# The FFN's down product as seven block products instead of plain accumulation, with its weight operands made a phase earlier

## The chip, the cores and the metric

One core of one Trainium2 chip runs the whole program. The metric is the device time of one execution in microseconds (us). A program's time is the median of several executions; one further execution was recorded by the hardware profiler, and all durations below are from that one.

## What is computed

One decoder layer on 1032 tokens (1024 of a prompt, 8 single samples), with model width 1024 and FFN width 2816. Cut to what the change touches:

```
x = x + 1/2 * SwiGLU_1(RMSNorm(x))     # gate, up = split(x @ w_in); (silu(gate) * up) @ w_out
x = x + token_mix(RMSNorm(x))          # attention and gated DeltaNet, one output projection
x = x + 1/2 * SwiGLU_2(RMSNorm(x))
y = RMSNorm(x)
```

The two FFNs have the same shapes. The change is in the last product of each, `(silu(gate) * up) @ w_out`: 2816 hidden features (22 blocks of 128) into 1024 model features (8 blocks of 128), for all 1032 tokens.

## The kernel before, in words

**Number format.** Every matrix product works on a pair of tiles, hi and lo: ScalarE casts the fp32 value to hi, VectorE subtracts hi from it to get lo (`split`, L250). A product is three matmuls, hi x hi, hi x lo and lo x hi, into one PSUM bank (`mm3`, L319). Activations are stored with features on the 128 partitions and tokens along the free dimension.

**Gate and up** (`ffn_in`, L651). The gate and up columns of one block f of hidden features are two block rows, the tokens are cut into two halves p = 0, 1 and each half into two quarters of 258 columns, and the 2x2x2 block product is done with seven block products in place of eight (Strassen's scheme in Winograd's form). The operands of the tokens are made once for all f (`x_ops`) and hold 28 of the 44 work tiles (`SLOTS`) until the last f. Those of the weights are made for every f (`w_ops`, L478): GpSimd makes four sums or differences of 128x512, ScalarE and VectorE split seven of them into hi and lo; `A_LIVE` = 9 of these tiles may be alive. `product` (L519) issues 12 matmuls of 258 columns for each of the seven and each half. `swiglu` (L536) empties the banks on VectorE and ScalarE, multiplies on GpSimd, and writes the result h to memory (the DRAM tile `hd`).

**Down** (`ffn_out`, L706). h comes back by block (`h_tile`, L677: one load of 128x1032, one cast, one subtraction). The 22 blocks of hidden features are taken in five groups (`KGROUPS`, L37: 4, 4, 6, 4 and 4). For every group, output block m and chunk of 344 tokens, the group's blocks are accumulated in one bank and VectorE adds half of it to the residual x (`one`, L709). The weights are loaded as they stand in memory and split (`issue`, L296). Nothing but loads, casts, subtractions on VectorE and these additions goes on beside it. The last group of four runs chunk by chunk, with the norm that follows behind it.

**What sets the order.** TensorE runs in the order in which the program is written (`ORDERED`). Where another engine's instruction stands in its queue is decided by a scheduler that plays the program on a timeline of its own; once it stands there, each queue is worked in order. All DMAs named here are issued by SP's queue. Work tiles come from one list of 44 slots: a tile's first writer waits for the last user of the slot before. `adv` (L418) steps the builders of operands between products; a builder steps on while the free slots it asks for (`room`) are there.

## Time and profile before

| what | value |
|---|---|
| median of 3 runs | 2116.67 us (2114.2 to 2116.69) |
| the profiled execution: its time | 2115.43 us |
| the profiled execution: first to last instruction | 2113.2 us |
| TensorE (PE) busy, matmuls | 96% of the span, 15062 |
| VectorE (DVE), ScalarE (ACT), GpSimd (POOL) busy | 58%, 33%, 28% |
| mean granted TensorE clock | 0.973 of full speed |
| DMA over the span | 86 GB/s |

The gate-and-up phases fill about 139 to 509 us and 1465 to 1849 us of the span, the down products the 249 us behind each. In the rows below, a group reads: line, engine, operation, out<-in by the program's names, sizes, count | busy us, mean ns of one | idle time before it and what ended it. In a timeline row the first two numbers are start and duration in us. In a row of windows, each engine has its busy us and (x) its number of instructions; the last three columns are the granted TensorE clock, the DMA engines' mean busy share and GB/s. PEld is TensorE's weight load.

### The profile page before, as it was taken

What the parts mean: (1) busy time and instruction counts of PE and PEld (TensorE: products, weight loads), DVE (VectorE), ACT (ScalarE), POOL (GpSimd) and SP (SyncE); (2) the same over time, 40 slices, a digit from 0 to 9 for tenths busy, and PEclk for the clock granted to TensorE, in tenths of its full rate; (3) what the DMA queues carried; (4) which work ended last, traced back from release to release, by engine and by line L of the source; (5) the groups of instructions that cost most, each with busy time, mean ns of one, the idle gap of its engine ahead of it and who ended that gap; (6) DMA issues with size and microseconds to landing.
All of it is one profiled execution on the core that took longest, in us unless ns stands there. A gap on an engine that the chain in (4) does not pass through costs nothing.

```text
span 2113.2 us, 37138 instructions
## 1 busy us (share of the span) xinstructions
PE 2024.6 (96%) x15062; PEld 1963.6 (93%) x15062; DVE 1222.1 (58%) x2624; ACT 699.8 (33%) x1491; POOL 594.9 (28%) x517
## 2 busy tenths in 40 slices
PE   7799999999999999999999979999999999999997
PEld 6799999999999998787888869899999999999997
DVE  7755555555533544676977874685555555464335
ACT  5233333333211333545243332443333333331112
POOL 3354444341000131332211111245444444200003
PEclk7999999999999999999999979999999999999999
DMA  4112222227322221211212151221222222552112
GB/s 152 60 58 91 81 73 84 86 71 281 113 68 60 84 81 35 69 45 32 67 46 50 57 181 35 97 70 61 86 81 83 79 81 76 194 195 84 55 41 81
DMA packets 109771, 180.81 MB, mean 86 GB/s; under 512 B 35168, under 2 KB 63744, under 8 KB 109584
## 3 DMA queue, kind: packets, MB, share of 16 engines
q1 hardware_dynamic: 109568, 178.41, 26.6%
q8 instruction: 118, 1.93, 0.4%
q14 instruction: 53, 0.43, 0.1%
q0 software_dynamic: 32, 0.03, 0.0%
HBM read 135.60 MB, written 43.85 MB: 85 GB/s over the span
## 4 chain that ended last, share of the span: by engine, by line
PE 40%; DVE 8%; DMA 1%; issue 1%; SPq 1%; ACT 0%; POOL 0%; DVEq 0%; ACTq 0%; POOLq 0%
PE mm L321 6%; PE mm L322 6%; PE mm L323 6%; PE ps L528 4%; PE ps L530 4%; PE ps L529 4%; PE ps L243 3%; PE mm L528 2%; PE mm L530 2%; PE mm L529 2%; DVE conv L89 1%; DVE inv L89 1%; SPq L102 1%; DVE Tb L89 1%; DVE x L89 1%
## 5 line engine op out<-in xcount | busy, mean ns | idle before, releaser
L528 PE MATMUL ps<-xhi,wop 128*128 128x258 f32 x1480 | 421.0, 284 | 7.4 <-DVE sw L89 7.2
L530 PE MATMUL ps<-xhi,wop 128*128 128x258 f32 x1480 | 419.3, 283 | 0.0
L529 PE MATMUL ps<-xlo,wop 128*128 128x258 f32 x1480 | 419.3, 283 | 0.0
L321 PE MATMUL mm<-hhi,hi 128*128 128x344 f32 x1008 | 322.3, 320 | 0.0
L322 PE MATMUL mm<-hlo,hi 128*128 128x344 f32 x1008 | 322.3, 320 | 0.0
L323 PE MATMUL mm<-hhi,lo 128*128 128x344 f32 x1008 | 321.6, 319 | 0.0
L89 DVE TENSOR_TENSOR wop<-r,wop 128x512 fp32r<-128x512 f32 x185 | 158.5, 859 | 253.9 <-ACT wop L89 239.8
L528 PEld LDWEIGHTS ps<-xhi,wop 128*128 128x128 f32 x1480 | 280.9, 190 | 8.7 <-issue 7.2
L529 PEld LDWEIGHTS ps<-xlo,wop 128*128 128x128 f32 x1480 | 281.9, 191 | 0.0
L530 PEld LDWEIGHTS ps<-xhi,wop 128*128 128x128 f32 x1480 | 281.2, 190 | 0.0
L89 DVE SCALAR_TENSOR_TENSOR x<-mm,x 128x344 f32<-128x344 f32 x240 | 123.3, 515 | 220.0 <-PE mm L323 217.9
L89 ACT CAST hi<-raw 128x1024 fp32r<-128x1024 f32 (+1 forms) x78 | 76.7, 984 | 357.0 <-PE mm L322 327.0
L321 PEld LDWEIGHTS mm<-hhi,hi 128*128 128x128 f32 x1008 | 189.4, 188 | 0.3 <-DVE x L89 0.3
L323 PEld LDWEIGHTS mm<-hhi,lo 128*128 128x128 f32 x1008 | 189.4, 188 | 0.0
L322 PEld LDWEIGHTS mm<-hlo,hi 128*128 128x128 f32 x1008 | 189.3, 188 | 0.0
L89 POOL TENSOR_TENSOR acc<-acc,t 128x344 f32<-128x344 f32 (+1 forms) x50 | 45.5, 911 | 508.2 <-ACT t L89 495.9
L321 PE MATMUL mm<-xnhi,hi 128*128 128x344 f32 x488 | 172.1, 353 | 0.0
L528 PE MATMUL mm<-xhi,wop 128*128 128x258 f32 x592 | 167.5, 283 | 0.0
L530 PE MATMUL mm<-xhi,wop 128*128 128x258 f32 x592 | 167.2, 283 | 0.0
L529 PE MATMUL mm<-xlo,wop 128*128 128x258 f32 x592 | 167.0, 282 | 0.0
L89 ACT CAST wop<-r 128x512 fp32r<-128x512 f32 x185 | 114.7, 621 | 144.6 <-PE mm L530 77.0
L323 PE MATMUL mm<-xnhi,lo 128*128 128x344 f32 x488 | 158.6, 325 | 0.0
(320 smaller groups left out, 4607.5 us busy)
## 6 DMA issues: line engine op xcount, KB each, us to landing
r<-in_w_in SPq DMA_DIRECT2D x86, 512.0 KB, 3.6
hraw<-hd SPq DMA_DIRECT2D x44, 516.0 KB, 5.0
hd<-sw SPq DMA_DIRECT2D x74, 258.0 KB, 2.0
raw<-in_w_out SPq DMA_DIRECT2D x34, 512.0 KB, 4.0
raw<-in_w_mix SPq DMA_DIRECT2D x22, 512.0 KB, 3.6
raw<-in_w_out SPq DMA_DIRECT2D x24, 384.0 KB, 3.2
x<-in_x SPq DMA_DIRECT2D x16, 516.0 KB, 9.0
xd<-x SPq DMA_DIRECT2D x24, 172.0 KB, 1.9
```

Source lines behind the costliest of these rows:

```text
L89: return fn(out, *a, **k)
L102: return self.eng.dma_start(out, src)
L243: self.nc.tensor.matmul(out, lhsT, rhs, start=start, stop=stop)
L321: mm(ps, whi, xhi, start=start, stop=False)
L322: mm(ps, whi, xlo, start=False, stop=False)
L323: mm(ps, wlo, xhi, start=False, stop=stop)
L528: mm(ps, w[:, a], x[0][:, c], start=first, stop=False, skip_group_check=True)
L529: mm(ps, w[:, a], x[1][:, c], start=False, stop=False, skip_group_check=True)
L530: mm(ps, wlo, x[0][:, c], start=False, stop=last, skip_group_check=True)
```

## The change

Eighteen of the 22 hidden blocks go through seven block products, in three groups of six blocks (`SGROUPS`, KG = 3 blocks to a half); the last four blocks (`REST`) stay as they were. A group is: for each pair j of output blocks, seven products; for each product both token halves p; for each half 9 matmuls of 258 columns, that is (hi x hi, hi x lo, lo x hi) for three blocks. A half's products run through three banks (`OUT_BANK`), and after every product VectorE adds half of the bank's running sum to one quarter of x (`OUT_TO`).

The weight operands of a pair j and a group (seven tiles of 128x768, hi and lo of 384 columns) are made by a paced builder (`wb_ops`) while gate and up runs: two loads, four sums or differences on GpSimd, seven splits, and each finished tile is stored to memory. There are 12 such pairs in an FFN. In the down product they are loaded again, one load of 384 KB for each product, up to eight alive. While this goes on, gate and up may have 6 weight tiles alive instead of 9.

The operands of h are made group by group in the down product (`h_ops`): for each half four loads of 128x3x258 (the tiles `hraw`), then for each of the seven products and each half one cast on ScalarE (128x774), two subtractions on VectorE (128x258 and 128x516) into tiles `hop`, and for the products 1, 2, 4 and 6 first a subtraction of 128x774 on GpSimd. The 21 hop tiles of a group are handed back one product at a time during the group's last pair j.

```diff
+KG = 3
+SGROUPS = [f * 2 * KG for f in range(3)]
+REST = len(SGROUPS) * 2 * KG
+OUT_BANK = (0, 1, 0, 2, 0, 1, 0)
+OUT_TO = ((0, 0), (1, 1), (0, 1), (0, 0), (1, 1), (0, 1), (1, 0))
+B_LIVE = 8
+A_LATE = 6
+PACE = 2900.0
+    def wb_ops(self, s1, s2, n, out):
...
+        def op(i, x):
+            yield from turn(PACE)
+            yield from self.room(1)
+            t = self.bt([P, 2 * n], F32R, "bop")
+            self.split(t[:, a], t[:, b], x)
+            late.append((i, t))
+            store(1)
+            yield True
...
+            if f == head + PREP_AT and 1 in ps:
+                self.limit = A_LATE
+                self.prepare_out(w_out)
...
+    def h_ops(self, hd, f0, out):
...
+        for i in range(7):
+            yield from room(3)
+            ts = [self.bt([P, 4 * HW], F32R, "hop") for _ in range(3)]
+            views = []
+            for p, r in enumerate(raws):
+                t = (0, 0)
+                if i in (1, 2):
+                    tt(r[t], r[(0, 1) if i == 1 else (1, 1)], r[t], ALU.subtract)
+                elif i == 4:
+                    tt(r[0, 1], r[1, 1], r[0, 1], ALU.subtract)
+                elif i == 6:
+                    tt(r[1, 0], r[1, 0], r[t], ALU.subtract)
+                x = r[(t, t, t, (1, 0), (0, 1), (1, 1), (1, 0))[i]]
+                hi, lo = ts[p][:, :n], [ts[p][:, n:], ts[2][:, p * e:(p + 1) * e]]
+                self.nc.scalar.copy(hi, x)
+                f = hi.bitcast(F32)
+                self.nc.vector.tensor_tensor(lo[0], x[:, :HW], f[:, :HW], ALU.subtract)
+                self.nc.vector.tensor_tensor(lo[1], x[:, HW:], f[:, HW:], ALU.subtract)
...
     def ffn_out(self, last_cb):
         nc = self.nc
+        for hb, wb in zip(self.hb, self.wb):
+            for j, ws in enumerate(wb):
+                banks = [], []
+                self.pair = max(self.pair, j)
+                for i in range(7):
+                    w = self.need_op(ws, i)
+                    views, ts = self.need_op(hb, i)
+                    for p in range(2):
+                        ps = self.out_product(i, w, views[p], banks[p])
+                        r, l = OUT_TO[i]
+                        x = self.need_op(self.xr, 2 * j + r)
+                        c0 = (2 * p + l) * HW
+                        x = x[:, c0:c0 + HW]
+                        with self.tc.high_priority(FIRST):
+                            nc.vector.scalar_tensor_tensor(x, ps, 0.5, x, ALU.mult, ALU.add)
+                    self.fr(w)
+                    self.alive -= 1
+                    if j == KT // 2 - 1:
+                        self.fr(*ts)
...
-        for f0, g in KGROUPS:
-            per = PER[g]
-            if f0 + g < NF:
...
```

**Three places in the queues.** First, VectorE in the middle of the first FFN's down product. Before, a run of additions x<-mm with a split (hlo, lo) now and then:

```order
L89 TENSOR_TENSOR hlo_6024<-hraw_6021,hhi_6023 128x1032
L89 SCALAR_TENSOR_TENSOR x_5559<-mm_5841,x_5559 128x344
L89 SCALAR_TENSOR_TENSOR x_5559<-mm_5855,x_5559 128x344
L89 SCALAR_TENSOR_TENSOR x_5561<-mm_5869,x_5561 128x344
L89 SCALAR_TENSOR_TENSOR x_5561<-mm_5883,x_5561 128x344
L89 SCALAR_TENSOR_TENSOR x_5561<-mm_5897,x_5561 128x344
L89 TENSOR_TENSOR lo_5914<-raw_5911,hi_5913 128x1024
L89 SCALAR_TENSOR_TENSOR x_5595<-mm_5917,x_5595 128x344
L89 SCALAR_TENSOR_TENSOR x_5595<-mm_5931,x_5595 128x344
```

Now, in the last pair of the first group, where the second group's operands are made (hraw_61.. is the first half's raw block of the new group, hraw_67.. the second half's; x_65.. is the residual that the old group still adds to):

```order
L101 TENSOR_TENSOR hop_6764<-hraw_6700,hop_6764 128x258
L101 TENSOR_TENSOR hop_6765<-hraw_6700,hop_6764 128x516
L101 SCALAR_TENSOR_TENSOR x_6538<-ps_6687,x_6538 128x258
L101 TENSOR_TENSOR hop_6862<-hraw_6178,hop_6862 128x258
L101 SCALAR_TENSOR_TENSOR x_6536<-mm_6708,x_6536 128x258
L101 TENSOR_TENSOR hop_6864<-hraw_6178,hop_6862 128x516
L101 TENSOR_TENSOR hop_6832<-hraw_6706,hop_6832 128x258
L101 TENSOR_TENSOR hop_6833<-hraw_6706,hop_6832 128x516
L101 SCALAR_TENSOR_TENSOR x_6536<-mm_6719,x_6536 128x258
L101 TENSOR_TENSOR hop_6874<-hraw_6704,hop_6874 128x258
L101 TENSOR_TENSOR hop_6875<-hraw_6704,hop_6874 128x516
L101 SCALAR_TENSOR_TENSOR x_6538<-ps_6676,x_6538 128x258
```

Each addition now has one or two splits of the next group ahead of it. The last row empties the bank of the first half's product 6, the last of the old group.

Second, GpSimd at the same place. Before, nothing stands between the last products of swiglu (sw) and the sums of squares (acc) at the end of the down product:

```order
L89 TENSOR_TENSOR sw_5371<-sw_5371,t_536_5372 128x258
L89 TENSOR_TENSOR sw_5386<-sw_5386,t_538_5387 128x258
L89 TENSOR_TENSOR sw_5371<-sw_5371 128x258
L89 TENSOR_TENSOR sw_5386<-sw_5386 128x258
L89 TENSOR_TENSOR acc_7321<-acc_7321,t_795_7374 128x344
```

Now there are eight subtractions for each group; these are the second half's four of the first group behind the last swiglu, and the eight of the second group:

```order
L101 TENSOR_TENSOR hraw_5943<-hraw_5945,hraw_5943 128x774
L101 TENSOR_TENSOR hraw_5945<-hraw_5947,hraw_5945 128x774
L101 TENSOR_TENSOR hraw_5943<-hraw_5947,hraw_5943 128x774
L101 TENSOR_TENSOR hraw_5949<-hraw_5949,hraw_5943 128x774
L101 TENSOR_TENSOR hraw_6176<-hraw_6178,hraw_6176 128x774
L101 TENSOR_TENSOR hraw_6700<-hraw_6702,hraw_6700 128x774
L101 TENSOR_TENSOR hraw_6178<-hraw_6180,hraw_6178 128x774
L101 TENSOR_TENSOR hraw_6702<-hraw_6704,hraw_6702 128x774
L101 TENSOR_TENSOR hraw_6176<-hraw_6180,hraw_6176 128x774
L101 TENSOR_TENSOR hraw_6700<-hraw_6704,hraw_6700 128x774
L101 TENSOR_TENSOR hraw_6182<-hraw_6182,hraw_6176 128x774
L101 TENSOR_TENSOR hraw_6706<-hraw_6706,hraw_6700 128x774
```

The engine's queue in the down product has gone from empty to eight instructions a group, for the products 1, 1, 4, 4, 2, 2, 6 and 6 in that order.

Third, SP's queue where gate and up of the first FFN ends. Before, loads of h (hraw) and of weights (raw) as they stand in memory:

```order
L102 DMA hraw_5347<-hd_160 128x1032
L102 DMA raw_5421<-in_w_out 128x2x512
L102 DMA hd_160<-sw_5142 128x516
L102 DMA hd_160<-sw_5157 128x516
L102 DMA hraw_5457<-hd_160 128x1032
L102 DMA raw_5415<-in_w_out 128x2x512
```

Now (bw is a weight operand in memory, bop the tile it is stored from, wb the tile it is loaded to):

```order
L114 DMA bw_5939<-bop_5893 128x768
L114 DMA wb_6031<-bw_1828 128x768
L114 DMA bw_5984<-bop_5936 128x768
L114 DMA wb_6070<-bw_1863 128x768
L114 DMA wb_6109<-bw_1634 128x768
L114 DMA wb_6163<-bw_2020 128x768
L114 DMA hraw_5943<-hd_160 128x3x258
```

The load of the second half's first raw block (hraw_5943, from which its operands of the products 0, 1 and 2 are made) stands behind the last stores of weight operands and behind the load wb_6163, whose slot is handed back by product 5 of the last f.

221 lines of the change are left out of this document (170 added, 51 removed).

## The prediction

> **What bounds the kernel now.** I read the windows first, one of the gate-and-up phase and one of the down product in each FFN.
>
> ```profile
> span 2113.2 us, 37138 instructions
> core 0: us, PE busy (x) PEld busy (x) DVE busy (x) ACT busy (x) POOL busy (x), PEclk, DMA share, GB/s
> 300.00:400.00 100.00, 100.00 (x835) 100.00 (x834) 54.12 (x85) 31.97 (x65) 44.45 (x40) 1.00 0.24 79
> 590.00:690.00 100.00, 100.00 (x638) 100.00 (x637) 37.48 (x56) 14.49 (x15) 0.00 (x0) 1.00 0.23 68
> 1500.00:1600.00 100.00, 100.00 (x834) 99.95 (x833) 53.91 (x84) 32.62 (x66) 45.49 (x42) 1.00 0.25 82
> 1910.00:2010.00 100.00, 100.00 (x639) 100.00 (x638) 38.25 (x57) 15.12 (x16) 0.00 (x0) 1.00 0.22 64
> ```
>
> In all four TensorE never waits and runs at full clock, so only fewer or cheaper matmuls shorten these stages, and any wait of TensorE lengthens them. The price of a matmul is a window over its count: 100/834.5 = 0.1198 us for 258 columns (gate and up), 100/638.5 = 0.1566 us for 344 (down). Next I read which engine could come late. POOL is idle in the down product and DVE at 38%; in gate and up they are at 45% and 54%. How these two get on together is in the timelines of POOL and DVE.
>
> ```profile
> 322.06 1.29 POOL L89 TENSOR_TENSOR ws<-ws,r 128x512 f32<-128x512 f32 x1 [1.68 <-DMA r<-in_w_in]
> 323.31 1.75 POOL L89 TENSOR_TENSOR r<-r,r 128x512 f32<-128x512 f32 x1
> 325.02 1.89 POOL L89 TENSOR_TENSOR sw<-sw,t 128x258 f32<-128x258 f32 x2
> 326.88 0.64 POOL L89 TENSOR_TENSOR sw<-sw 128x258 f32<-128x258 f32 x1
> ```
>
> ```profile
> 322.60 1.30 DVE L89 TENSOR_TENSOR wop<-r,wop 128x512 fp32r<-128x512 f32 x1 [3.37 <-ACT wop L89]
> 323.82 0.41 DVE L89 TENSOR_TENSOR sw<-ps,sw 128x258 f32<-128x258 f32 x1
> 324.16 1.45 DVE L89 TENSOR_TENSOR wop<-ws,wop 128x512 fp32r<-128x512 f32 x1
> 325.53 0.41 DVE L89 TENSOR_TENSOR sw<-ps,sw 128x258 f32<-128x258 f32 x1
> ```
>
> DVE's split begun at 322.60 ends 0.55 us after POOL's first sum (323.35). POOL's next runs 1.75 us in place of 1.29, the 0.46 longer that DVE still worked. The split begun at 324.16 ends 0.55 us after that sum (325.06), and POOL's next two take 1.89 us, 0.61 more than twice 0.64. So a split (two operands in SBUF) and a POOL sum take turns, whole instructions at a time, while the reading of a bank (sw<-ps) in the middle of it keeps its 0.41 us. The Trainium skill, page SBUF — State Buffer, section Who interferes with whom, calls this an exclusive lock on a shared port; the trace agrees (0.55 us left each time).
>
> **The matmuls.** Of 22 blocks 18 change. Before: 18 x 8 output blocks x 3 chunks x 3 = 1296 matmuls of 344 columns, 1296 x 0.1566 = 203.0 us an FFN. After: 3 groups x 4 pairs x 7 products x 2 halves x 9 = 1512 of 258, x 0.1198 = 181.1 us. That is -21.9 us an FFN, **-43.8 us** in all, if TensorE keeps this pace. A half product is 9 x 0.1198 = 1.08 us.
>
> **The operands at a change of group** (two in each FFN). Durations:
>
> ```profile
> L89 DVE TENSOR_TENSOR acc<-sq 128x258 f32<-128x258 f32 x4 | 1.7, 418 | 0.0
> L89 DVE TENSOR_TENSOR sq<-sq 128x516 f32<-128x516 f32 x4 | 2.7, 685 | 2.3 <-POOL sq L89 2.3
> L89 DVE TENSOR_TENSOR sw<-ps,sw 128x258 f32<-128x258 f32 x222 | 92.4, 420 | 31.1 <-PE ps L530 29.8
> L89 DVE TENSOR_TENSOR hlo<-hraw,hhi 128x1032 fp32r<-128x1032 f32 x44 | 53.6, 1229 | 28.5 <-ACT hhi L89 28.3
> L89 ACT CAST hi<-raw 128x768 fp32r<-128x768 f32 x24 | 20.0, 835 | 127.8 <-PE mm L322 121.2 <-issue 6.5
> L89 POOL TENSOR_TENSOR t<-x,t 128x1032 f32<-128x1032 f32 x4 | 9.6, 2400 | 0.2
> ```
>
> A pair of subtractions on DVE (258 and 516 columns) is 0.42 + 0.69 = 1.10 us, an addition to x 0.42, a cast 0.84. POOL at 774 columns lies between 1.29 (512) and 2.40 (1032): 1.85 us, an estimate. A group needs 14 pairs (15.4 us) and 8 POOL subtractions (14.8 us), and by the timelines these 30.2 us take turns.
>
> The new group's tiles come free as the old group's last pair j goes through. Product 0's are free 12 half products before the change (-13.0 us), its first cast is done at -12.1. The piece of VectorE's queue shown above ends with the addition that empties the bank of the old group's last product, first half. The new group's second half product takes that bank and wants it at +1.1. Between -12.1 and this addition the queue holds 8 pairs (8.8 us), and POOL's eight subtractions, which stand in its queue with nothing between, take their turns in the gaps (14.8 us); most of the additions run under POOL. That ends at -12.1 + 8.8 + 14.8 = +11.5: TensorE is 10.4 us late. Bounds: without any turn-taking 8.8 us of pairs and 11 additions (4.6) end at +1.3, and the operands of product 2, behind five POOL subtractions and their casts, are some 2.5 us late; if the last three pairs too had to be waited for, 13. I take 10.5, four times: **+42 us**. Before, nothing of the kind stood there.
>
> **The way into the down product** (once in each FFN).
>
> ```profile
> hraw<-hd SPq DMA_DIRECT2D x44, 516.0 KB, 5.0
> raw<-in_w_out SPq DMA_DIRECT2D x24, 384.0 KB, 3.2
> 500.00:520.00 20.00, 19.67 (x142) 19.47 (x141) 11.73 (x19) 7.73 (x10) 2.79 (x4) 1.00 1.02 408
> ```
>
> Before, this passage cost 0.33 us (20 - 19.67). Now, in the first FFN, the raw block hraw_5943 is asked for when product 5 of the last f ends, 2.9 us before the phase does; 5.0 later, at +2.1, it is there. Two casts (to +3.3, the queue has one ahead), a pair (+4.4), POOL for product 1 (+6.2), where POOL's next takes the port (+8.1), a pair (+9.2), POOL for product 2 (+11.1), a cast (+11.9). Ahead of its pair stand two pairs, two additions and one more turn of POOL (+15.4). TensorE wants this at 5 half products, +5.4: 10 late. In the second FFN the same chain is that of the first half and hangs behind the swiglu of the last f; counted in the same way it is 11 late. Bounds: 3 (the chain of load and cast alone, the rest in time) and 12. I take 10, twice: **+20 us**.
>
> **Into the last four blocks.** The fourth block of h reuses the second's raw tile: asked for some 3.5 us before the end of the groups, landed at +1.5, cast and split (1.05 and 1.23) at +3.3 to 3.8, wanted at +1.6 to 2. **+3.4 us** for both, between 0 and 10.
>
> **The clock after a wait.**
>
> ```profile
> 147.17 0.36 PE L528 MATMUL ps<-xhi,wop 128*128 128x258 f32 x1 [3.03 <-DVE sw L89]
> 147.17:151.00 3.83, 3.83 (x19) 3.83 (x20) 0.57 (x1) 0.62 (x1) 3.83 (x5) 0.56 0.10 37
> ```
>
> After a wait of 3.03 us the granted clock is 0.56 and 19 matmuls take 3.83 us, where 32 would fit: 13 x 0.12 = 1.5 us. At a change of group the last wait, for the bank, is some 6 us long: 4 x 1.5 = **+6 us**. The Trainium skill, page TensorE: Matmul & The Clock Gate, section HAM oscillation, warns of idle gaps over some 3.4 us; by that the shorter waits on the way into the product would cost nothing more, by the row a gap of 3.03 is enough and they would add up to 3 us each. I keep 6, bounds 3 and 12.
>
> **Gate and up.** One f takes 168 x 0.1198 = 20.1 us. Now the port is held for 7 splits (4.8 us, 0.69 each) and POOL's 4 x 1.29 + 4 x 0.64 = 7.7 us, 12.5 in all. 12 pairs of weights over 18 f add, for each f, two thirds of 7 splits of 384 columns (some 0.55 each) and 4 sums (some 0.97): 5.2 us, 17.7 of 20.1. The banks' 10 additions (4.2 us) run beside POOL. It fits, and 6 weight tiles alive are 17 us ahead; so TensorE goes on: 0, with an upper bound of 1 us a step, 36 us. The casts (some 0.7 x 7 x 2/3 = 3.3 us on ACT's 32%) hide. The bytes: 384 KB per 2.16 us are 182 GB/s, with raw blocks some 235, against 408 that the window from 500 shows; SP issues two or three DMAs in that time. Cover gone, that is the last rival.
>
> **Sum.** -43.8 + 42 + 20 + 3.4 + 6 = +27.6 us on the profiled execution's 2115.4 (span 2113.2 and 2.2 around it): 2143.0. The median of the runs lies 1.2 us above that execution, inside their spread; I leave it: **2143 us**. Its own range, with 8 to 13 for each change of group and 7 to 12 for each way in, is 2125 to 2168.
>
> **Rivals.** *The operands are in time* (faster). DVE's splits get their turns early, POOL's subtractions run late and only product 2 waits: 2.5 us at each of the six places, and no long gap: -43.8 + 15 + 3.4 = -25, 2090 us. For it speak the shares: DVE 38% and POOL 0% in the down product. The Trainium skill, page Perfetto Trace Analysis, section Identifying the Most-Contended Engine, judges such engines by occupancy; by that rule the operands hide and this rival, or its extreme of 2072, is the outcome. Against it: the sum of both engines' work is what counts at the port, and 30.2 us do not fit between -12.1 and +13 (product 6's turn). It decides at a delay of 7 us a place: below that the change gains. 0.23. *The six places take about 7 us each*: 2112 to 2121, 0.06. *Gate and up fills the port*: the queues stand in an unlucky order, each f loses up to 1 us, +36 on top: 2179. For it: 17.7 of 20.1 us; against: 17 us of lead. 0.08. *The stored weights come late* (the change does not stream as it says): SP's queue stands behind a raw load and each product takes 2.5 us in place of 2.16: 168 x 0.34 = +57, 2200 us. Against: eight tiles alive. 0.05. My forecast has 0.58.
>
> The range 2086 to 2172 leaves out the best part of the first rival and the last two, some 0.2. A measurement can tell about 0.2% (4 us) from no change: faster 0.23, same 0.06, slower 0.71.
>
> **What would show it.** Right: at each change of group, PE waits of 8 to 13 us on DVE additions and hop tiles; DVE pairs of 1.1 us stretched towards 3 with POOL busy; a half-clock window behind; 835 matmuls per 100 us inside the pairs j = 1 and 2 and in gate and up. Wrong: PE at 100% through the changes of group, or POOL subtractions that do not stretch the pairs; then the time is near 2090. PE below 100% between 200 and 450 us would be the third rival, PE waiting on DMA the last.

## The result and the profile after

The changed kernel takes 2208.66 us (median of 4 runs, 2202.19 to 2210.12), the kernel before 2115.43 in the same rounds (2113.77 to 2116.69): a ratio of 1.0435, 95% interval 1.0412 to 1.0458. The sign was forecast, the size was not: +93 us against +27.6, outside the range. The profiled execution after has a span of 2206.1 us (before 2113.2), and all stages below are from such spans. The times of the first and last matmul of each line group give the length of each stage:

| stage, us | before | after | difference | forecast |
|---|---|---|---|---|
| gate and up by seven products, first FFN | 369.4 | 398.6 | +29.2 | 0 |
| down, the 18 changed blocks, first FFN | 203.9 | 217.8 | +13.9 | +12.1 |
| down, last four blocks, first FFN | 45.6 | 49.5 | +3.9 | +1.7 |
| gate and up, second FFN | 389.6 | 420.5 | +30.9 | 0 |
| down, the 18 blocks, second FFN | 203.9 | 221.0 | +17.1 | +12.1 |
| down, last four, second FFN | 47.9 | 48.0 | +0.1 | +1.7 |
| everything else | 852.8 | 850.7 | -2.1 | 0 |

(Forecast for 18 blocks: half of -43.8 + 42 + 20 + 6.) So the down products came out 35 us longer, near the 27.6 forecast for them. The other 60 us are in the phases where the weights' operands are made, which the forecast held at nothing.

The windows that answer to those of before, same columns (busy us and count of PE, PEld, DVE, ACT, POOL; granted clock, DMA share, GB/s):

```profile
300.00:400.00 100.00, 93.22 (x751) 92.81 (x750) 64.59 (x104) 41.01 (x86) 52.88 (x48) 0.97 0.56 195
590.00:690.00 100.00, 89.84 (x689) 88.82 (x688) 68.70 (x115) 20.93 (x26) 29.80 (x15) 0.92 0.63 195
1500.00:1600.00 100.00, 91.98 (x731) 90.94 (x730) 64.28 (x96) 37.36 (x77) 55.64 (x48) 0.97 0.47 160
1910.00:2010.00 100.00, 87.11 (x640) 84.90 (x640) 66.44 (x106) 21.81 (x30) 34.99 (x20) 0.88 0.74 237
```

In gate and up there are now 751 and 731 matmuls in 100 us where 835 and 834 stood, TensorE waits for 7 to 8% of the time, and its clock is no longer full (0.97). That was the sign named for the third rival. Over both gate-and-up phases TensorE's idle time before its matmuls adds up to 47.0 us, before to 7.4. That is some 40 of the 60 us; the other 20 are slower matmuls, at a mean clock of 0.97 and 0.98 in the two phases, before 1.00.

**What TensorE waits for in gate and up.** A selection of the waits from 140 to 537 us of the kernel after (engine, what waited, for whom: us in total, times, longest):

```profile
DVE wop L101 <- ACT wop L101: 61.7, 48, 4.1
ACT wop L101 <- DMA bw<-bop: 44.2, 23, 4.9
ACT wop L101 <- DMA r<-in_w_in: 26.8, 9, 5.6
PE ps L594 <- DVE sw L101: 22.2, 12, 5.0
ACT sw L101 <- DMA hd<-sw: 18.4, 12, 4.7
```

and the same of the kernel before, from 140 to 509:

```profile
DVE wop L89 <- ACT wop L89: 120.4, 66, 4.6
ACT wop L89 <- PE mm L530: 37.9, 27, 2.3
ACT wop L89 <- DMA r<-in_w_in: 8.3, 13, 3.5
ACT sw L89 <- DMA hd<-sw: 5.5, 4, 2.2
PE ps L528 <- DVE sw L89: 3.4, 2, 3.0
```

TensorE hardly waits for a weight tile (wop, 1.3 us); it waits for the emptying of a bank (sw): 22.2 us in place of 3.4. VectorE has less idle time in front of its splits than before, even with the 36.0 us in front of the new ones (bop). What changed is whom ScalarE's casts (wop) wait for: before mostly TensorE, that is, a product that has to be over anyway; now a store's landing (44.2) and a raw load (26.8). The row `ACT sw` is no cast: it is ScalarE's copy of the first product's bank into a fresh tile sw, and it waits 18.4 us, before 5.5, for stores of h (hd<-sw). This copy matters. In `swiglu` the eviction of the next bank on VectorE adds that bank to the copy, so it cannot begin before the copy is done.

One gap shows how this reaches TensorE: SP, ScalarE, VectorE and PE of the kernel after, around 1730 us (start, duration; in brackets the idle time before and its releaser):

```profile
1726.29 0.33 SPq L114 DMA_DIRECT2D r<-in_w_in  x1
```

```profile
1731.84 0.62 ACT L101 CAST wop<-r 128x512 fp32r<-128x512 f32 x1 [3.80 <-DMA r<-in_w_in]
1733.20 1.14 ACT L101 CAST wop<-ws 128x512 fp32r<-128x512 f32 x2 [0.74 <-POOL ws L101]
1734.25 0.37 ACT L101 COPY sw<-ps 128x258 f32<-128x258 f32 x1
```

```profile
1732.49 1.23 DVE L101 TENSOR_TENSOR wop<-r,wop 128x512 fp32r<-128x512 f32 x1 [3.92 <-ACT wop L101]
1733.85 2.14 DVE L101 TENSOR_TENSOR wop<-ws,wop 128x512 fp32r<-128x512 f32 x2
1735.92 0.41 DVE L101 TENSOR_TENSOR sw<-ps,sw 128x258 f32<-128x258 f32 x1
```

```profile
1736.38 0.58 PE L594 MATMUL ps<-xhi,wop 128*128 128x258 f32 x1 [3.85 <-DVE sw L101]
```

SP sends the raw load at 1726.29, between stores of weight operands. ScalarE stands still for 3.80 us until it has landed, VectorE for 3.92 until the cast is done. Then the work for later products goes first in both queues: three casts ahead of ScalarE's copy, three splits, beside GpSimd's sums, ahead of VectorE's eviction. The bank that TensorE has wanted since 1732.53 is read at 1735.92. ScalarE's queue alone would have held it until the copy ended at 1734.62; VectorE's adds the last 1.3 us.

In a third of the gaps VectorE's queue is not in the way at all:

```profile
303.00 0.38 ACT L101 COPY sw<-ps 128x258 f32<-128x258 f32 x1 [1.40 <-DMA hd<-sw]
303.40 0.43 DVE L101 TENSOR_TENSOR sw<-ps,sw 128x258 f32<-128x258 f32 x1 [0.83 <-ACT sw L101]
303.88 0.39 PE L594 MATMUL ps<-xhi,wop 128*128 128x258 f32 x1 [2.15 <-DVE sw L101]
```

The copy waits for the landing of a store of h, VectorE stands idle until the copy is done, and TensorE until the eviction is. The two phases have 26 gaps of over 0.3 us that an eviction ends. In 9 of them (13.5 us) VectorE was idle like this right before the eviction, and in all nine the copy had waited for a store of h. Counted gap by gap, a copy that was not yet done accounts for 20.2 us of the 47, and an eviction that was ready and stood behind other work in VectorE's queue for 11.7; most of the rest is the evictions' own time.

**The changes of group**, forecast at 12 us each with their clock. The 126 matmuls of a pair j take 15.1 us when nothing waits; the pairs of the two FFNs after:

```
first FFN   28.4 15.1 15.1 19.7 | 22.4 15.1 15.1 19.7 | 21.7 15.1 15.1 15.2
second FFN  32.4 15.1 15.1 19.7 | 21.7 15.1 15.1 19.7 | 21.8 15.1 15.1 15.1
```

What lies over 15.1 on both sides of a bar is 11.9, 11.2, 11.2 and 11.3 us: 45.6 for the four. The first pair of each FFN is 13.3 and 17.3 longer. VectorE, GpSimd and TensorE at the first change (601.8 to 624.2):

```profile
607.48 1.73 DVE L101 TENSOR_TENSOR hop<-hraw,hop 128x258 fp32r<-128x258 f32 x1
609.13 0.41 DVE L101 SCALAR_TENSOR_TENSOR x<-ps,x 128x258 f32<-128x258 f32 x1
609.47 2.95 DVE L101 TENSOR_TENSOR hop<-hraw,hop 128x516 fp32r<-128x516 f32 x3
612.34 0.41 DVE L101 SCALAR_TENSOR_TENSOR x<-ps,x 128x258 f32<-128x258 f32 x1
...
623.29 0.41 DVE L101 SCALAR_TENSOR_TENSOR x<-ps,x 128x258 f32<-128x258 f32 x1
```

```profile
602.81 8.11 POOL L101 TENSOR_TENSOR hraw<-hraw,hraw 128x774 f32<-128x774 f32 x4 [1.02 <-DVE hop L101]
612.56 3.83 POOL L101 TENSOR_TENSOR hraw<-hraw,hraw 128x774 f32<-128x774 f32 x2 [1.64 <-DVE hop L101]
```

```profile
609.60 0.39 PE L876 MATMUL ps<-hop,wb 128*128 128x258 f32 x1 [1.20 <-DVE x L101]
612.81 0.58 PE L876 MATMUL ps<-hop,wb 128*128 128x258 f32 x1 [1.86 <-DVE x L101]
623.81 0.55 PE L876 MATMUL ps<-hop,wb 128*128 128x258 f32 x1 [3.96 <-issue]
```

VectorE's subtraction of 128x258, 0.44 us on the mean without GpSimd's work (e8 and e12 below), takes 1.73 here beside GpSimd. The additions stand behind such subtractions, and TensorE goes on 0.5 us after the additions at 609.13, 612.34 and 623.29 have begun (for the third wait the profile names no releaser). Here the wait comes in pieces, not as the one long wait that the prediction drew, but it is the same queue and the same turn-taking. The pieces add up to 24.4 us for the four changes; the other 21.2 of the 45.6 are matmuls at a lower clock, 0.88 on the mean over the pairs on both sides of a bar.

The first pairs wait for operands of h, as in this row, the longest of the first FFN:

```profile
541.66 0.58 PE L876 MATMUL ps<-hop,wb 128*128 128x258 f32 x1 [3.73 <-ACT hop L101]
```

### The profile page after: what moved, and what is told of

Read it like the earlier page. It is cut to its first block, busy times and chain, and to the rows that moved or that the text cites. A ratio compares the mean times of both kernels' runs of the same rounds, so it can differ in the third digit from the quotient of the medians.

```text
span 2206.1 us, 40029 instructions
## 1 busy us (share of the span) xinstructions
PE 2034.5 (92%) x15494; PEld 1961.6 (89%) x15494; DVE 1416.4 (64%) x3028; ACT 757.7 (34%) x1667; POOL 791.7 (36%) x661
## 4 chain that ended last, share of the span: by engine, by line
PE 29%; DVE 10%; DMA 7%; issue 3%; ACT 1%; SPq 1%; POOL 1%; DVEq 0%; ACTq 0%; POOLq 0%
PE mm L333 3%; PE mm L334 3%; PE mm L335 3%; PE ps L255 3%; PE ps L594 2%; PE ps L596 2%; PE ps L595 2%; PE ps L877 2%; PE ps L876 2%; PE ps L878 2%; DMA r<-in_w_in 2%; DMA hd<-sw 2%; DMA bw<-bop 2%; DVE bop L101 1%; DVE hop L101 1%
## 5 line engine op out<-in xcount | busy, mean ns | idle before, releaser
L594 PE MATMUL ps<-xhi,wop 128*128 128x258 f32 x1480 | 430.1, 291 | 44.0 <-DVE sw L101 43.7
L596 PE MATMUL ps<-xhi,wop 128*128 128x258 f32 x1480 | 425.7, 288 | 3.0 <-DVE wop L101 2.9
L594 PEld LDWEIGHTS ps<-xhi,wop 128*128 128x128 f32 x1480 | 287.5, 194 | 50.2 <-DVE sw L101 50.0
L596 PEld LDWEIGHTS ps<-xhi,wop 128*128 128x128 f32 x1480 | 287.3, 194 | 3.8 <-DVE wop L101 3.8
L101 DVE TENSOR_TENSOR wop<-r,wop 128x512 fp32r<-128x512 f32 x185 | 172.3, 939 | 123.3 <-ACT wop L101 123.0
L876 PE MATMUL ps<-hop,wb 128*128 128x258 f32 x720 | 216.3, 300 | 30.9 <-DVE x L101 12.3
L877 PE MATMUL ps<-hop,wb 128*128 128x258 f32 x720 | 216.1, 300 | 5.6 <-DVE hop L101 5.5
L878 PE MATMUL ps<-hop,wb 128*128 128x258 f32 x720 | 213.6, 297 | 0.0
L101 POOL TENSOR_TENSOR hraw<-hraw,hraw 128x774 f32<-128x774 f32 x48 | 95.3, 2000 | 248.2 <-DVE hop L101 181.8
L876 PEld LDWEIGHTS ps<-hop,wb 128*128 128x128 f32 x720 | 147.1, 204 | 33.8 <-DVE x L101 14.0
L101 POOL TENSOR_TENSOR lo<-raw,hi 128x1024 fp32r<-128x1024 f32 (+1 forms) x30 | 67.6, 2254 | 298.0 <-ACT hi L101 285.2
L101 DVE SCALAR_TENSOR_TENSOR x<-ps,x 128x258 f32<-128x258 f32 x240 | 100.4, 423 | 112.5 <-PE ps L878 112.4
L101 ACT CAST hop<-hraw 128x774 fp32r<-128x774 f32 x84 | 67.7, 838 | 273.9 <-PE ps L877 185.0
L334 PE MATMUL mm<-xnlo,hi 128*128 128x344 f32 x488 | 157.2, 322 | 0.0
```

What stands on the lines that cost most here:

```text
L101: return fn(out, *a, **k)
L334: mm(ps, whi, xlo, start=False, stop=False)
L594: mm(ps, w[:, a], x[0][:, c], start=first, stop=False, skip_group_check=True)
L596: mm(ps, wlo, x[0][:, c], start=False, stop=last, skip_group_check=True)
L876: mm(ps, a, x[0][k], start=i in (0, 1, 3) and k == 0, stop=False, skip_group_check=True)
L877: mm(ps, a, x[1][k], start=False, stop=False, skip_group_check=True)
```

## The experiments

The theories. *Down product*: the port that VectorE and GpSimd share decides (the prediction's chain), against the place of the evictions in VectorE's queue alone. *Gate and up*: the port (third rival of the prediction); the bytes and landing times of the stores and loads; too few slots (a tile gets a slot just given back); too little lead; SP's queue. Each kernel was timed in 3 rounds beside the kernel before. The last columns are the stages of both FFNs together, from the profiles.

| run | us | ratio to before | gate and up | 18 down blocks |
|---|---|---|---|---|
| before | 2115.43 | 1 | 759.0 | 407.8 |
| after | 2208.66 | 1.0435 [1.0412, 1.0458] | 819.1 | 438.8 |
| e1 one pair made | 2154.15 | 1.0188 [1.0165, 1.0211] | 768.2 | 433.5 |
| e2 no stores | 2178.35 | 1.0305 [1.0279, 1.0332] | 792.1 | 434.8 |
| e3 no sums | 2208.22 | 1.0449 [1.0428, 1.0469] | 814.3 | 441.9 |
| e4 before, slots held | 2115.95 | 1.0020 [1.0005, 1.0034] | 759.3 | 408.1 |
| e5 stores of another tile | 2243.54 | 1.0608 [1.0580, 1.0636] | 776.4 | 437.5 |
| e6 no casts, splits, stores | 2172.86 | 1.0262 [1.0243, 1.0282] | 775.1 | 441.2 |
| e7 limit 4 | 2239.62 | 1.0572 [1.0538, 1.0605] | 829.9 | 446.0 |
| e8 e1, no subtractions of h | 2098.23 | 0.9907 [0.9891, 0.9924] | 767.7 | 375.9 |
| e9 stores of 48 KB | 2197.03 | 1.0391 [1.0363, 1.0418] | 806.2 | 436.2 |
| e10 limit 7 | 2247.85 | 1.0633 [1.0602, 1.0664] | 824.2 | 475.6 |
| e11 e1, B_LIVE 4 | 2140.22 | 1.0116 [1.0092, 1.0140] | 778.2 | 411.1 |
| e12 e1, subtractions by VectorE | 2123.37 | 1.0038 [1.0019, 1.0057] | 766.5 | 403.3 |
| e14 four slots more | 2249.13 | 1.0640 [1.0603, 1.0677] | 880.3 | 415.6 |
| e15 four more, limit 8 | 2192.99 | 1.0365 [1.0334, 1.0396] | 825.9 | 417.0 |
| e16 mended down product | 2173.89 | 1.0283 [1.0250, 1.0315] | 821.2 | 406.7 |
| e17 splits by GpSimd | 2233.11 | 1.0557 [1.0521, 1.0593] | 832.3 | 444.0 |
| e18 e16, stores by ScalarE's queue | 2188.77 | 1.0358 [1.0325, 1.0392] | 837.8 | 405.8 |
| e19 e16, splits later | 2203.69 | 1.0436 [1.0399, 1.0473] | 830.7 | 421.4 |

One caution for small differences: e1, e8, e11 and e12 make the same one pair of weights in gate and up (and keep the limit of 9 weight tiles), and have 766.5 to 778.2 us there. A different order of the same work is worth some 10 us of the two phases, in e2 and e5 16. The stages are read from one execution of each kernel.

### The two halves of the loss apart

**e1.** The diff:

```diff
-                self.limit = A_LATE
                 self.prepare_out(w_out)
...
+                    if f0 == 0 and j == 0:
-                    yield from self.wb_ops(...)
+                        yield from self.wb_ops(...)
...
+        self.wd = [[self.wd[0][0]] * (KT // 2) for _ in SGROUPS]
```

> The changed kernel, but only the first of the 12 pairs of weight operands is made and stored in each gate-and-up phase, and the limit of gate and up's own weight tiles stays at 9; all 84 loads of the down product read this one pair's seven stored tiles again (so the down product computes with wrong weights). The stage table of the two traces gives the 18 blocks of the down product +13.9 and +17.1 us, the last four blocks +3.9 and 0.0, the gate-and-up phases +29.2 and +30.9. If the two parts of the loss are independent, as all theories of the gate-and-up phase have it, this run has the first part alone: 2115 + 35 = 2150 us, 2145 to 2160 with one pair's making left in. Rival: the down product is late because its first weights are still being made when it begins; then it loses less here, below 2135.

2154: the two halves are nearly independent. Without the making of the weights the 18 blocks still take 433.5 us (after 438.8), so it is not weights still being made that hold up the down product. The rival falls. That it is the operands of h, the next run shows.

### The down product

**e8**, on e1: the four `tt(r[..], ...)` of `h_ops` taken out.

> As the run with one pair made (2154 us), and without GpSimd's subtractions of 128x774 in the down product; the raw blocks are cast and split in their place (wrong operands of h). By the prediction's chain the 14.8 us of subtractions hold the port and stand in the way of each change of group: without them the pairs end at about +1.3 instead of +11.5, each of the 4 changes costs 0 to 3 us instead of 10, each of the 2 ways in about 5 instead of 10, and the clock term goes: 2095 to 2115, under the kernel before. Rival (the late bank is due to the place of its eviction in VectorE's queue and to tiles that come free one product at a time, whatever GpSimd does): 2135 or more.

2098, under the kernel before. The pairs on both sides of a change are 15.1 to 15.3 us: each change now costs 0.2 in place of 11.2 in e1, and the first pair of each FFN nothing. The second pair of each FFN is 6 us longer than the others, in e1 1.7: TensorE waits there once, 4.4 us, for an addition to x in front of which VectorE stands idle 3.51 us until a load has landed. So the way in falls from 13.0 and 12.2 us to 6, and what is left is no longer the operands of h. The stretch of the first change, which in e8 lies from 566.23 to 588.63 us, with TensorE busy throughout:

```profile
566.23:588.63 22.40, 22.40 (x188) 22.32 (x187) 20.65 (x49) 11.17 (x14) 0.00 (x0) 1.00 0.90 296
```

**e12**, on e1: `tt = self.nc.vector.tensor_tensor` in `h_ops`.

> As the run with one pair made (2154 us), with GpSimd's subtractions of 128x774 in the down product done by VectorE instead (nothing is left out of them). VectorE takes 0.69 us for 512 columns of the kind, so some 1.03 for 774 (an estimate), 8.2 us for 8 of them in place of 14.8 on GpSimd, and nothing takes turns: 23.6 us of work at a change of group in place of 30.2. Port theory: 6.6 us less at each of the six places, 2110 to 2130. Rival (the work just stands in VectorE's queue ahead of the bank's eviction, whoever did it before): no gain, 2145 or more.

2123, inside what the port theory expected, but not spread as it said (6.6 us at each of six places): a change costs 3 us less than in e1, a way in 8 to 9. The groups of VectorE's subtractions and the subtractions of 774 columns, in the kernel after, in e8 and in e12 (busy us, mean ns of one | idle before):

```profile
L101 POOL TENSOR_TENSOR hraw<-hraw,hraw 128x774 f32<-128x774 f32 x48 | 95.3, 2000 | 248.2 <-DVE hop L101 181.8 <-DMA hraw<-hd 54.3 <-DMA wb<-bw 8.0
L101 DVE TENSOR_TENSOR hop<-hraw,hop 128x516 fp32r<-128x516 f32 x84 | 87.0, 1036 | 0.0
L101 DVE TENSOR_TENSOR hop<-hraw,hop 128x258 fp32r<-128x258 f32 x84 | 66.0, 786 | 10.6 <-ACT hop L101 10.2 <-DMA hraw<-hd 0.3
```

```profile
L101 DVE TENSOR_TENSOR hop<-hraw,hop 128x516 fp32r<-128x516 f32 x84 | 58.6, 697 | 0.5 <-PE mm L596 0.5
L101 DVE TENSOR_TENSOR hop<-hraw,hop 128x258 fp32r<-128x258 f32 x84 | 37.6, 447 | 12.0 <-ACT hop L101 12.0
```

```profile
L101 DVE TENSOR_TENSOR hop<-hraw,hop 128x516 fp32r<-128x516 f32 x84 | 60.5, 720 | 0.0
L101 DVE TENSOR_TENSOR hraw<-hraw,hraw 128x774 f32<-128x774 f32 x48 | 46.1, 964 | 0.0
L101 DVE TENSOR_TENSOR hop<-hraw,hop 128x258 fp32r<-128x258 f32 x84 | 36.1, 435 | 8.0 <-ACT hop L101 8.0
```

With GpSimd in the down product, VectorE's 168 subtractions are busy for 153.0 us, without it for 96.2 (e8) and 96.6 (e12). The 48 subtractions themselves take 95.3 us on GpSimd and 46.1 on VectorE. The Trainium skill's exclusive lock (page SBUF — State Buffer, section Who interferes with whom) agrees with the stretched subtractions. e12 keeps 7.8 to 8.5 of the 11.2 us at each change, and there all that work stands in VectorE's queue within one pair, with nothing on GpSimd. So at the changes the rival holds for the larger part: the amount of work ahead of the additions counts for about 8 us, and that GpSimd does it, slower and in turns with VectorE, for about 3.

**e11**, on e1: `B_LIVE = 4` for 8.

> As the run with one pair made (2154 us), with B_LIVE = 4 in place of 8: the down product keeps 4 of its weight tiles alive, and with the slots that frees the 8 raw blocks of the next group are loaded, and product 0's operands made, some 45 half products (48 us) before the change of group in place of 12. By the prediction's chain 2 of the 14 pairs and 2 of the 8 subtractions of GpSimd (6 us of the port) then go ahead of the last pair: each change costs some 5 us less, the ways in 2 to 5 less, 2118 to 2138. Rival: four weight tiles are too few (an operand every 2.16 us, 3.6 to land), or the order of the rest decides: 2150 or more.

2140, just over the expected band; but its gate and up took 10 us longer than e1's, and the 18 blocks gained 22. The ways in fall from 13.0 and 12.2 us (the first two pairs, over 15.1 each) to 5.1 and 2.9, and the first change of each FFN by 2.8 and 3.5; the second does not (12.5 and 11.7, in e1 11.0 and 11.3). So most of it is at the ways in, where the expectation had the smaller part. Four weight tiles alive were enough.

**e16**, the kernel after, complete, with e11's and e12's edits.

> The changed kernel, complete, with B_LIVE = 4 and the subtractions of h done by VectorE. Each of the two alone took 14 and 31 us off the run with one pair; if they add up, 2208 - 45 = 2163, between 2155 and 2178 us, since both shorten the same passage. The gate-and-up loss stays.

2174, inside 2155 to 2178: the 18 blocks lost 32 us, and gate and up stayed (821.2 against 819.1). This is the best complete version of the seven products that was found. It stays 2.8% behind the kernel before, all of it now in gate and up.

### Gate and up: what the loss grows with

**e3**, `wb_ops` without its four `tt(...)`:

> The changed kernel without GpSimd's four sums for each pair of down weights (96 of them in all); raw pieces are cast, split and stored in their place (wrong weights). Port theory: without 96 x 1 us and the turns that splits lose by them, gate and up gets most of its 60 us back, 2175 or less. Slot theory and transfer theory: the splits, the slots and the stores are the same, 2190 to 2205.

2208, 5 us less in the two phases. The third rival of the prediction named the right place; of its cause, the work on the port, the new sums are worth 5 of the 60 us, which is within the caution above. The time lies just over the band of the slot and transfer theories.

**e2**, all but the first pair's stores left out:

```diff
-                d = self.dram.tile(...)
-                nc.sync.dma_start(d, t.bitcast(F32))
+                if not out[i]:
+                    d = self.dram.tile(...)
+                    nc.sync.dma_start(d, t.bitcast(F32))
+                    out[i] = d
                 self.fr(t)
-                out[i] = d
...
+        self.wd = [[self.wd[0][0]] * (KT // 2) for _ in SGROUPS]
```

> The changed kernel with all casts, sums and splits of the weight operands, but only the first pair's seven tiles are stored; the other 77 tiles are given back as soon as they are split, and all loads of the down product read the first pair's tiles (wrong weights). Port theory (the third rival of the prediction: VectorE's splits and GpSimd's sums take turns and fill the time): nothing on the port changes, 2200 us or more. Transfer theory (raw loads and slots wait for 64 MB of stores, in SP's queue and on the way): most of the 60 us of the two gate-and-up phases come back, 2165 or less. Slot theory (tiles get a slot that was given back a product or less before, and their splits stand in VectorE's queue ahead of the evictions): the waits for a store's landing go, those for a product's end and for raw loads stay, 2170 to 2195.

2178, in the band of the slot theory: 27 of the 60 us come back.

**e5** puts `self.other`, a token operand, in the place of the stored tile:

> The changed kernel with all 84 stores of 384 KB in each FFN, but each stores a token operand that stays in its tile through the phase in place of the tile just split, which is given back at once (wrong weights). The stores' bytes and their places in SP's queue are the same; no store waits for a split, and no slot waits for a store. If the 30 us that the run without stores got back come from the bytes (contention on the way to memory), 2200 to 2210 us. If they come from tiles that wait for a store's landing, and from SP's queue standing behind a split, about as without stores: 2175 to 2188.

2244, but not as meant: with nothing to wait for, the stores were put ahead of the phase, where the stretches before gate and up grew by 34 and 44 us; no store is left in the phase itself. It tells nothing of bytes against waits. Its gate and up, 776.4, is one more reading of e2's work, 16 us lower.

**e9**, from the second pair on `t.bitcast(F32)[:, :96]` is stored, 48 KB for 384:

> The changed kernel with all 84 stores in each FFN at their places, each waiting for its split and holding its slot until it has landed, but from the second pair on each stores 96 of its 768 columns, 48 KB in place of 384 (all loads of the down product read the first pair's tiles: wrong weights). It replaces the run that stored another tile, whose stores went ahead of the phase (the stretch before each gate and up got 34 and 44 us longer in it, and no store stands in the phase). If the stores cost by their bytes, 2172 to 2186 us, as without stores. If they cost by SP standing behind a split and by slots that wait for a landing, 2195 to 2208.

2197, in the band for waits, near its lower end: 13 us of the phases go with the bytes, 14 with the stores' being there at all; that split is no finer than the caution allows. The landing times, from 150 to 500 us, before and after (SP's queue, count, KB, median us from issue to landing):

```profile
r<-in_w_in SPq DMA_DIRECT2D x32, 512.0 KB, 3.6
hd<-sw SPq DMA_DIRECT2D x34, 258.0 KB, 2.0
```

```profile
r<-in_w_in SPq DMA_DIRECT2D x33, 512.0 KB, 4.3
hd<-sw SPq DMA_DIRECT2D x32, 258.0 KB, 3.9
```

**e6**, `if out[i]: yield True; return` ahead of each cast and split:

> The changed kernel without the casts, splits, tiles and stores of the down weights behind the first pair: only the 24 loads of 384 KB and the sums of GpSimd remain of their making (wrong weights). The run without stores kept 16.5 us of gate-and-up loss in each FFN, and the run with one pair 4.6. If these 12 us are casts and splits whose tiles get slots given back in the same product, the loss falls to that of one pair and the time to 2150 to 2160. If they are the loads (SP's queue, raw tiles that take slots), 2170 to 2180.

2173, in the band for the loads; but the stages say otherwise. Gate and up is 775.1, 7 us over e1, and the rest of the time lies outside it (the 18 blocks 8 longer than e1, the stretches outside all products 4). So the other 77 casts and splits of each FFN are worth up to 17 us, loads and sums 7.

Added up, for the two phases: 759 before; 768 with one pair; 775 with all loads and sums; 792 with casts and splits (776 in e5's order); 806 with small stores; 819 with whole ones. No one item makes the 60 us, and the steps between neighbours are hardly larger than what order alone is worth.

### Gate and up: is one resource short?

**e4**, the kernel before with `held = [self.slots.pop(0) for _ in range(4)]` and the limit at 6 through the phase:

> The kernel before, with nothing of the change, but 4 of the 44 work slots are held unused through gate and up (from the second full step to the last but one) and its weight tiles are limited to 6: a weight tile then gets a slot that was given back 2 products before (median) in place of 4, as in the changed kernel. Slot theory: splits stand in VectorE's queue ahead of evictions that the products wait for, gate and up gets 5 to 15 us longer in each FFN, 2125 to 2145. Port theory and transfer theory: no work and no byte is added, 2115 within 4 us.

759.3 against 759.0: quick reuse of slots alone costs nothing when nothing else is added. The slot theory had expected 5 to 15 a phase.

**e7 and e10**, `A_LATE = 4` and `A_LATE = 7`:

> The changed kernel with A_LATE = 4 in place of 6: gate and up keeps 4 weight tiles alive, and two more slots go round. A down-weight tile then gets a slot given back 2 products before (median) in place of the same product. Slot theory: gate and up gets back a good part of its 60 us, 2165 to 2192. Rival (the lead of gate and up's own weights is what is short): their splits are later still, 2212 or more. Transfer theory by bytes alone: 2208 within 5.

> The changed kernel with A_LATE = 7 in place of 6; with 4 it took 2240 us in place of 2208. Lead theory (raw blocks land late, so what counts is how far ahead gate and up's own operands are made): a tile more of lead, 2190 to 2203. Slot theory: the weight tiles now get slots given back in the same product (median 0, before 2), so 2212 to 2235.

Both are slower. e7 falls into the band of the lead theory and e10 far from it, above that of the slot theory too: neither has both. Gate and up moves little (830, 819, 824 for 4, 6, 7). e10 pays in the down product, 475.6: the making of the weights reaches into it (casts of bop stand there), and TensorE waits up to 9.5 us for operands of h; e7 has 11 in gate and up, 7 in the down product and some 3 elsewhere; its profiled execution (2229.6) is the fastest of its four, 10 us under their median. With four tiles alive TensorE also waits for weight tiles, 12.1 us in the two phases, after 2.9.

**e14 and e15**, four slots more from the second full step on, with limits 6 and 8:

```diff
+            if f == head + 1:
+                for x in xT:
+                    self.fr(*x[6])
+                    x[6] = x[5]
...
-                    if f == NF - 1:
+                    if f == NF - 1 and i != 5:
```

> The changed kernel with 4 more slots in gate and up: from the second full step on the token operands of the seventh product are given back and the sixth's are used in their place (so the seventh product computes with wrong tokens; no work of the phase is left out). Limit 6 as in the changed kernel; a down-weight tile then gets a slot given back 4 products before (median, in place of the same product), a weight tile of gate and up 6 (in place of 2). Slot theory: half or more of the 60 us of the two phases comes back, 2150 to 2180. Rival (what stands in VectorE's queue and SP's queue decides, whichever slot it uses): 2195 to 2210.

> The same 4 slots more, and A_LATE = 8: they are used for more of gate and up's own tiles instead of for later reuse (down-weight tiles 2 products, weight tiles 4, as in the kernel before). If both slots and lead are short, as the runs with limits 4 and 7 say (both slower than 6), 2150 to 2180; if reuse alone is, worse than with limit 6; if neither, 2195 to 2210.

2249 and 2193; 880 and 826 in gate and up: more slots give nothing back, and with limit 6 they cost 61 more. The slot theory falls as an account of the time. (In both runs the down product is some 22 us shorter than after, at the ways in, and e15 is faster than the kernel after for it. Why was not followed up.) What the slots were to cure is gone in e14: late copies of the first bank account for 0.8 us of its waits, after 20.2. In their place evictions that are ready stand behind other work in VectorE's queue for 67.2 us, after 11.7. A gap of e14, on VectorE and on TensorE:

```profile
433.88 1.66 DVE L101 TENSOR_TENSOR wop<-r,wop 128x512 fp32r<-128x512 f32 x1 [4.44 <-ACT wop L101]
...
438.69 0.68 DVE L101 TENSOR_TENSOR wop<-ws,wop 128x512 fp32r<-128x512 f32 x1
439.29 0.41 DVE L101 TENSOR_TENSOR sw<-ps,sw 128x258 f32<-128x258 f32 x1
```

```profile
439.76 0.58 PE L594 MATMUL ps<-xhi,wop 128*128 128x258 f32 x1 [3.98 <-DVE sw L101]
```

VectorE stands still for 4.44 us at a split whose cast is late (the cast waits for a raw load and for a store's landing that comes 0.95 us after it), and then works off four splits, beside GpSimd's sums, before the eviction. That free slots put more splits ahead of the evictions is a reading of these waits, not shown by a run of its own.

**e17**, the 84 splits of down weights on GpSimd:

> The changed kernel, complete, with the 84 splits of the down weights in each FFN done by GpSimd in place of VectorE. Queue theory: the evictions that the products wait for stand behind these splits in VectorE's queue, and each split behind its cast, its slot and its load; out of that queue, a third or more of the 60 us comes back, 2165 to 2190. Slot theory alone: gate and up's own splits still wait for slots that stores hold, 2200 or more, and GpSimd's sums come later on top.

2233, in the band of the slot theory, gate and up 13 longer than after. VectorE's queue is rid of them and stands longer behind ScalarE's other casts (87.7 us at wop from 160 to 500, after 58.4). TensorE's waits show why little could come back: in 17 gaps (34.7 us, after 13.5 in 9) VectorE was idle right before the eviction and waited for ScalarE's copy.

**e18**, `self.tc.nc.scalar.dma_start(d, ...)` for the stores, on e16:

> The complete kernel with both mended pieces of the down product (2174 us), and the 84 stores of the down weights in each FFN issued by ScalarE's queue in place of SP's. SP theory: SP stands behind a split for each store (126 us of waits in the first phase of the changed kernel), and the raw loads of gate and up and the stores of h, which free the tiles that the evictions write, are issued late behind it. Then 15 to 30 of the 61 us of gate-and-up loss come back: 2144 to 2160. Rival (VectorE's queue order and the bytes decide): 2168 to 2180; or ScalarE now stands behind the splits and its casts are late: 2185 or more.

2189, in the last band, gate and up 17 longer than in e16. SP is free of the stores, and the waits for raw loads and for the store of h are still there (36.7 and 15.7 us in the first phase, 26.8 and 18.4 after). But now ScalarE's queue stands behind the splits: late copies of the first bank account for 36.7 us of the waits of both phases, in e16 for 19.7. So freeing SP brings nothing back in this way; that SP's standing behind the splits costs nothing is not shown, since the standing only moved to ScalarE.

**e19**, 4 us more between each raw load and its first cast, on e16:

> The complete kernel with both mended pieces of the down product (2174 us), and 4 us more in the program's own count of time between each load of raw weights (gate and up's, and the down weights') and the first cast and split of it, so that these stand later in the queues of ScalarE and VectorE. Order theory: VectorE stands less often at a split whose load has not landed, with evictions behind it: 2140 to 2160. Rival (the tiles are then ready later, and with 6 of them alive the lead is what is short): 2180 or more.

2204: the rival's side by its time. Gate and up is 10 longer, and the down product 15 longer as well. The rival's reason is not seen: TensorE waits for weight tiles 3.3 us in the two phases, hardly more than after (2.9).

## Why the prediction was right and wrong

**The matmuls**: forecast -43.8. 24 pairs at 15.1 us against 407.8 before: -45.4. Right.

**The change of group**: forecast 42, and 6 for the clock. Measured 45.6 together. The sum is right by luck, since two errors cancel: the waits are 24.4 us in place of 42, and the lower clock costs 21.2 in place of 6. The queue and the work in it are right: 0.2 us a change without GpSimd's subtractions (e8), about 8 with that work on VectorE (e12), 11.2 with it on GpSimd (e1). The shape is not: three waits of 1.2 to 4 us in place of one long one, with slow matmuls between and behind them.

**The way in**: forecast 20, measured 30.6. Right in kind (TensorE waits for hop casts and pairs in the first 15 to 20 us, and e8 takes these waits away), too small in size. The waits themselves are 6.8 and 9.9 us, under the forecast's 10 each; the rest of the 13.3 and 17.3 is the clock after them, in the first FFN 0.66 over the first 15.1 us, which the forecast had counted only at the changes of group.

**The last four blocks**: forecast 3.4, measured 4.0.

**Gate and up**: forecast 0, with an upper bound of 36. Measured +60.1, 1.67 us for each of the forecast's 36 steps. This is the step that failed, as the prediction put it: "It fits, and 6 weight tiles alive are 17 us ahead; so TensorE goes on". The 17 us of lead belong to the weight tiles, and TensorE hardly waits for these (2.9 us in the whole execution). It waits for evictions, which have no lead at all: ScalarE's copy of the first bank shares a queue with the casts and waits for a store of h, and VectorE's evictions share one with the splits. A cast that is late stops both queues, and the bank behind them. The sum of busy times could not show that: VectorE is at 64% and ScalarE at 41% in the window from 300. And behind some of the waits TensorE runs at a lower clock, for which the forecast had nothing here: some 40 us are waits, some 20 the clock.

What is shown: the place (the stages), the waits (evictions behind ScalarE's copy and behind splits, these behind loads and landings), and that leaving out the stores gives 27 us back. What is not: that a single cause stands behind the 60. More slots, more or less lead, another queue for the stores, no new sums and a later place of the splits were each tried, and none gave anything back but the sums' 5 us. That an order with the evictions ahead in both queues would is argued from the gaps above and wasn't tried. Taken gap by gap, VectorE's queue alone holds 11.7 of the 47 us of waits in the kernel after, so that order would have to be mended on ScalarE too.

**The rivals.** *Operands in time* is out: e8 is what it would have been (2098 with one pair made), and it takes the removal of the work on the port. The Trainium skill's reading by occupancy (page Perfetto Trace Analysis, section Identifying the Most-Contended Engine) would have kept it: VectorE 38% and GpSimd 0% busy before, and the four changes cost 45.6 us. *Stored weights come late* is out too: inside the pairs j = 1 and 2 no product waits.

## What to carry to other kernels

Work put on an engine that also empties TensorE's banks, here ScalarE as well as VectorE, is not free when its busy time fits: what counts is whether anything in its queue can stand still for a transfer while a bank waits behind it, and lead in the operands doesn't help there. Look at what the late eviction itself waited for before blaming its queue. Before giving a subtraction to an idle GpSimd, add its time to VectorE's two-operand work on the same stretch; here the same 48 subtractions done by VectorE took half the time and 31 us off the run with one pair made. A change that moves work to an earlier phase has to be priced in that phase too.

## What was not expected of the hardware

The length of one gap does not tell whether the clock falls. In gate and up of the kernel after, a gap of 2.04 us to 456.15 left TensorE at full clock, one of 1.99 us to 1670.23 did not. The clock's record tells why. In this execution every stretch at one clock, full or half, is a multiple of 3.41 us long (the last is cut off), so the clock changes only on a fixed grid of that step. Four steps of the grid, two around each gap:

```profile
452.17:455.59 3.42, 1.95 (x17) 1.73 (x15) 1.12 (x2) 1.63 (x4) 0.97 (x1) 1.00 0.96 357
455.59:459.00 3.41, 2.85 (x23) 2.85 (x24) 3.19 (x4) 2.22 (x5) 3.27 (x3) 1.00 0.49 193
1667.32:1670.73 3.41, 1.42 (x12) 1.21 (x11) 1.32 (x3) 0.89 (x2) 1.96 (x2) 1.00 0.82 278
1670.73:1674.14 3.41, 3.41 (x19) 3.41 (x18) 2.12 (x4) 2.17 (x4) 1.85 (x2) 0.50 0.61 220
```

The first gap is split by the grid into 1.47 and 0.57 us, the second lies within one step, and the next step runs at half clock: 19 matmuls where 30 ran in the one after. In the two gate-and-up phases of this execution a step at full clock with up to 1.47 us of idle TensorE was always followed by full clock, one with 1.90 us or more always by half. Two short gaps in one step add up: 1.20 us to 609.60 and 1.86 us to 612.81, at the first change of group, put 2.06 us of idle time into the step from 609.19, and the next ran at 0.50. The Trainium skill's limit of some 3.4 us for a gap (page TensorE: Matmul & The Clock Gate, section HAM oscillation) is too high for this kernel: 1.99 us was enough once. In the first gate and up of the kernel after, waits are 23.7 of the 398.6 us, and another 12.6 are lost beside them (3024 matmuls at 0.1198 us would take 362.3).
